# A hybrid recurrence and attention trunk on one core: the products of x1 with the compression, query and gate weights, as seven 2x2 block products in place of eight

## The chip, the cores and the metric

One core of a Trainium2 chip runs the whole program. The metric is the device time of one launch in microseconds (us), the median of the runs shown. Engines go by the profile's names: PE (TensorE) multiplies, DVE (VectorE) and ACT (ScalarE) do the elementwise work, POOL (GpSimd) and SP issue transfers (DMAs). Each engine takes its instructions in the program's order and waits on semaphores that others raise.

## The reference, cut to what matters

```python
x1 = x + rglru_layer(x, ...)                 # ends in y @ w_out_a
h  = rms_norm(x1, norm_kv)
ckr = h @ w_dkv                              # 256 columns for k and v, 64 for the rotated keys
c_kv = rms_norm(ckr[..., :256], kv_norm)
k_rope = apply_rope(ckr[..., 256:], cos, sin)
h  = rms_norm(x1, norm_b)
u  = h @ w_in_b                              # 384 query columns, 8 x 128 gate columns
c_q = rms_norm(u[..., :384], q_norm)
gate = u[..., 384:]
q  = c_q @ w_uq                              # 128 plain and 64 rotated columns for each of 8 heads
o  = causal attention over k = c_kv @ w_uk with k_rope, v = c_kv @ w_uv
out = rms_norm(x1 + (o * silu(gate)) @ w_out_b, final_norm)
```

Sequence 1024, model width 1024, recurrence width 1280, all in float32.

## The kernel before, in words

**Layout.** A tile holds 128 channels by the sequence, which is worked in two halves of 512 columns (`hs(h)`). To multiply float32 values, every operand is split in two parts by `hl` (lines 79 to 81): ACT copies it rounded (`hi`, line 80), DVE takes the difference (`lo`, line 81). A product of a 128x128 weight block with 128x512 data is then three matmuls (`mm3`, lines 111 to 114: hi*hi, hi*lo, lo*hi); `mmt` strings them over the 128-channel blocks k into one PSUM tile. Weights come through `wload` (line 83): a load by SP (line 89), a gain by DVE where one is wanted (line 93), then the split. Their raw tiles have 2 buffers, the parts 4. Large tiles are pages, 36 of 128x1024 in one pool.

**Phase A** is the recurrence; its ten results `ys` stand as 20 pages. The change leaves it alone.

**Phase B** (lines 457 to 491) makes x1 = x + y @ w_out_a, eight tiles of 128 channels by ten k-blocks. `out_a` (line 460) loads a piece of x (`xr`, 2 buffers), adds it to the PSUM tile (line 464), splits x1 into the pages `xs1` (line 465), stores x1 (line 466, POOL's queue) and adds its squares to `acc1`.

**Phase C** (lines 493 to 631) multiplies x1 by 14 weight tiles of 128 columns: 2 for k and v, 1 for the rotated keys, 3 query tiles, 8 gates. Each takes 2 halves x 8 k-blocks x 3 matmuls of 128x512. The row norm of x1 is a factor for each column, so it is applied behind the product (`byr`, line 160; `rstd`, line 137, makes the root). Between the products stand: the rotation of the keys (lines 556 to 575), the norms and splits of c_kv and c_q (`normed`, line 520), and the query rotation of two groups of four heads (lines 606 to 623), whose parts go to DRAM (`qsd`) to be read back for each head. Six gates follow the query rotation. A gate is sigmoid on ACT (line 597), times itself on DVE (line 598), stored to `gd`. The first weights of phase C are loaded and split while phase B still multiplies (`wq_`, `wnext`), and the first product takes 7 of its 8 k-blocks before the last tile of x1 is wanted.

**Attention** (line 633 on) goes head by head. Its PSUM pool `pss` is opened when phase C's pool `psp` closes, in the same banks. First come head 0's plain queries and keys (tiles `pm`, line 112 to 114 by `kq`), then the scores `s`, whose rotated part reads `qs`, loaded from `qsd`.

**What sets the order.** A scheduler orders each engine's instructions by their dependences and priorities when the program is built; `wload` raises the priority of weights by 100. A pool's memory that is given on (`pa.close()`, `pc.close()`) makes the next user wait for the last readers of what lay there.

## Time and profile before

| | us |
|---|---|
| median of 3 runs | 900.16 (900.0 to 900.78) |
| span of the profiled execution, first to last instruction | 896.9 |
| matmuls in the profile, PE busy | 4410, 874.6 |
| DVE busy, ACT busy | 645.0, 447.6 |

The profiled execution's own time is not given beside its span; the median lies 3.3 us above the span, and that difference is taken as what lies around it. Rows of groups read: line, engine, operation, written tile <- read tiles, shape and count, then busy us, mean ns of one, and the idle time before them with what ended it. Rows of stretches give for each engine the busy us and the instruction count, then the clock granted to PE. Timeline rows give the start, the length, and the instruction. A mean length is from start to end of one instruction; engines overlap the end of one with the start of the next, so the step from start to start is shorter.

### The profile page before, as it was taken

The page shows a single profiled execution, that of the slowest core. Times are in us where ns is not written, and L with a number is a line of the kernel's source. Part 1 is how long each engine was busy: PE and PEld are TensorE (multiplying, and loading weights), DVE is VectorE, ACT ScalarE, POOL GpSimd, SP SyncE. Part 2 cuts the span into 40 slices and gives each one's busy share as a digit, 9 for nine tenths or more (in the row PEclk, how much of TensorE's full clock was granted, in tenths as well). Part 3 has the DMA queues.
Part 4 walks back from the last instruction along what each step waited for, and adds up shares of the span by engine and source line. Part 5 has one row for each costly group of instructions (what it writes and reads, how often), then busy time and mean ns, then how long its engine had stood idle before and what let it go on. Part 6 is the DMA issues. An engine that isn't in the chain of part 4 may idle for free.

```text
span 896.9 us, 12070 instructions
## 1 busy us (share of the span) xinstructions
PE 874.6 (98%) x4410; PEld 743.4 (83%) x4410; DVE 645.0 (72%) x1192; ACT 447.6 (50%) x765; POOL 67.9 (8%) x125
## 2 busy tenths in 40 slices
PE   7999999999999999999999999999999999999993
PEld 5788888888887888888888888989998998888993
DVE  7988787777777545559599636978887887774552
ACT  6457777777787323233343225645565554331221
POOL 3001110011000100001003000000000000010000
PEclk9999999999999999999999999999999999999997
DMA  7333333333221644412125324223231317565131
GB/s 266 101 105 94 98 91 103 97 106 101 75 58 53 196 119 135 142 38 74 51 97 211 141 86 132 77 74 106 75 109 66 115 60 280 189 228 171 64 103 48
DMA packets 49612, 101.66 MB, mean 113 GB/s; under 512 B 6160, under 2 KB 16272, under 8 KB 49552
## 3 DMA queue, kind: packets, MB, share of 16 engines
q1 hardware_dynamic: 35952, 66.40, 23.3%
q0 software_dynamic: 13328, 34.22, 11.4%
q8 instruction: 35, 0.57, 0.3%
q10 hardware_dynamic: 272, 0.26, 0.1%
q14 instruction: 25, 0.20, 0.1%
HBM read 77.26 MB, written 23.07 MB: 112 GB/s over the span
## 4 chain that ended last, share of the span: by engine, by line
PE 70%; DVE 11%; issue 9%; ACT 6%; DMA 2%; POOL 1%; SPq 0%; DVEq 0%; POOLq 0%; ACTq 0%
PE ps L113 11%; PE ps L114 11%; PE ps L112 10%; PE pm L114 5%; PE pm L113 5%; PE pm L112 5%; PE pm L710 3%; DVE t L356 2%; PE pm L727 2%; PE pm L726 2%; PE s L691 2%; PE s L693 2%; PE s L694 2%; PE s L692 2%; PE pm L725 2%
## 5 line engine op out<-in xcount | busy, mean ns | idle before, releaser
L113 PE MATMUL ps<-pg,wh 128*128 128x512 f32 x728 | 284.2, 390 | 3.2 <-DVE pg L260 2.9
L112 PE MATMUL ps<-pg,wh 128*128 128x512 f32 x728 | 283.4, 390 | 2.0 <-ACT wh L80 1.3
L114 PE MATMUL ps<-pg,wl 128*128 128x512 f32 x728 | 283.7, 390 | 0.3 <-DVE wl L81 0.3
L113 PEld LDWEIGHTS ps<-pg,wh 128*128 128x128 f32 x728 | 136.7, 188 | 34.4 <-DVE pg L260 5.7
L112 PEld LDWEIGHTS ps<-pg,wh 128*128 128x128 f32 x728 | 136.6, 188 | 31.2 <-ACT wh L80 1.4
L114 PEld LDWEIGHTS ps<-pg,wl 128*128 128x128 f32 x728 | 136.7, 188 | 29.2 <-DVE wl L81 1.2
L80 ACT ACTIVATE wh<-wr 128x512 fp32r<-128x512 f32 (+2 forms) x85 | 48.3, 571 | 64.8 <-PE ps L113 48.4
L80 ACT ACTIVATE pt<-pm 128x512 fp32r<-128x512 f32 (+2 forms) x96 | 44.4, 490 | 59.4 <-PE pm L710 57.4
L81 DVE TENSOR_TENSOR wl<-wr,wh 128x512 fp32r<-128x512 f32 (+2 forms) x85 | 52.1, 615 | 27.4 <-ACT wh L80 27.0
L700 ACT ACTIVATE pg<-s,m 128x128 f32<-128x128 f32 (+3 forms) x64 | 47.5, 743 | 46.0 <-DVE m L697 41.2
L112 PE MATMUL pm<-pg,pg 128*128 128x256 f32 (+1 forms) x192 | 61.9, 323 | 0.0
L113 PE MATMUL pm<-pg,pg 128*128 128x256 f32 (+1 forms) x192 | 61.6, 321 | 0.0
L114 PE MATMUL pm<-pg,pg 128*128 128x256 f32 (+1 forms) x192 | 61.4, 320 | 0.0
L81 DVE TENSOR_TENSOR pt<-pm,pt 128x512 fp32r<-128x512 f32 (+2 forms) x96 | 50.6, 548 | 1.9 <-ACT pt L80 1.8
L697 DVE TENSOR_REDUCE m<-s 128x1 f32<-128x128 f32 (+3 forms) x64 | 48.1, 754 | 1.0
L80 ACT ACTIVATE pg<-pg 128x512 fp32r<-128x512 f32 x46 | 29.0, 632 | 39.3 <-DVE pg L410 17.8
L356 DVE SCALAR_TENSOR_TENSOR t<-xb,vec,t 128x512 f32<-128x512 f32 x60 | 44.7, 746 | 0.4
L710 PE MATMUL pm<-ident,pg 128*128 128x128 f32 x288 | 42.4, 274 | 0.3 <-DVE pg L702 0.3
L112 PEld LDWEIGHTS pm<-pg,pg 128*128 128x128 f32 x192 | 36.6, 191 | 2.6 <-issue 0.2
L113 PEld LDWEIGHTS pm<-pg,pg 128*128 128x128 f32 x192 | 36.6, 191 | 2.6 <-issue 0.2
L114 PEld LDWEIGHTS pm<-pg,pg 128*128 128x128 f32 x192 | 36.6, 191 | 2.5 <-DVE pg L756 0.3
L690 PE MATMUL s<-pg,pg 128*128 128x512 f32 (+2 forms) x96 | 37.1, 387 | 0.9 <-ACT pg L700 0.9
(188 smaller groups left out, 1611.9 us busy)
## 6 DMA issues: line engine op xcount, KB each, us to landing
wr<-wina SPq DMA_DIRECT2D x40, 256.0 KB, 2.8
wh<-wina POOLq DMA_DIRECT2D x36, 256.0 KB, 3.0
wr<-winc SPq DMA_DIRECT2D x28, 256.0 KB, 2.6
ysd<-pg POOLq DMA_DIRECT2D x12, 512.0 KB, 3.2
pg<-ysd SPq DMA_DIRECT2D x12, 512.0 KB, 8.2
wr<-wouta SPq DMA_DIRECT2D x16, 256.0 KB, 2.7
xr<-xT SPq DMA_DIRECT2D x16, 256.0 KB, 3.0
x1d<-t POOLq DMA_DIRECT2D x16, 256.0 KB, 3.4
```

The source lines that it names most:

```text
L80: A.activation(out=hi, in_=src, func=AF.Copy)
L81: V.tensor_tensor(out=lo, in0=src, in1=f(hi), op=ALU.subtract)
L112: T.matmul(out=ps, lhsT=w[0], rhs=r[0], start=first, stop=False)
L113: T.matmul(out=ps, lhsT=w[0], rhs=r[1], start=False, stop=False)
L114: T.matmul(out=ps, lhsT=w[1], rhs=r[0], start=False, stop=last)
L356: V.scalar_tensor_tensor(out=xc, in0=xb[:, j:j + HW], scalar=cwv[j], in1=xc, op0=ALU.mult, op1=ALU.add)
L690: T.matmul(out=sc[:, c], lhsT=q[0][:, ql], rhs=k[0][:, c], start=True, stop=False)
L691: T.matmul(out=sc[:, c], lhsT=q[0][:, ql], rhs=k[1][:, c], start=False, stop=False)
L692: T.matmul(out=sc[:, c], lhsT=q[1][:, ql], rhs=k[0][:, c], start=False, stop=False)
L697: V.tensor_reduce(out=m, in_=sc, axis=AX.X, op=ALU.max, negate=True)
L700: A.activation(out=p_[:, 0:nk], in_=sc, func=AF.Exp, bias=m, accum_out=l)
L710: T.transpose(out=ps[:, (b - b0) * P:(b - b0 + 1) * P], in_=p_[:, b * P:(b + 1) * P], identity=ident)
```

## The change

**Factors in place of x1's parts.** Phase B works the tiles of x1 in pairs (j, j+4). Of each pair and its two halves, four pieces b11, b12, b21, b22 of 128x512, `factors` makes seven operands (three of them differences, one a further sum, on DVE) and splits each into its `fx` pages, 28 pages in place of 16. The last pair (3, 7) is multiplied together, k-block by k-block in four PSUM tiles, so that the pages of `ys` come free one after the other.

**Weights in place.** `wpair` loads four 128x512 pieces of two weight tiles, puts the gain on with ACT (four instructions for each piece), makes the four combinations with DVE and splits seven operands. The tiles `wa` lie in a pool that opens when phase B's pool `ta` closes.

**Seven products in place of eight.** `pair` multiplies seven operands by seven, four k-blocks each, in four PSUM tiles, three of which take a second product on top of what they hold. DVE combines the results (`v2`, `u3` and lines 603 to 612) and applies the row norm. The first pair takes three of its four k-blocks first.

**Moved behind the gates:** the splits of c_q and c_kv (`parts`), the rotation of the keys with the loads of its tables, and the query rotation of the first four heads. The second group of the query rotation moves into the attention, in head 1. Gates use ACT's Silu in place.

```diff
-    xs1 = [(page(), page()) for _ in range(NKT)]
+    fx = [[None, None] for _ in range(7)]
...
+    def factors(j, b11, b12, b21, b22):
+        fput(0, j, b11)
+        t1 = diff(b11, b12, ALU.subtract)
+        fput(1, j, t1)
+        t2 = diff(b22, t1, ALU.add)
+        fput(2, j, t2)
+        fput(3, j, diff(b12, b22, ALU.subtract))
+        fput(4, j, b21)
+        fput(5, j, diff(b21, t2, ALU.subtract))
+        fput(6, j, b22)
...
+    def wblock(m, h):
+        t = tcp.tile([P, HW], F32, tag="wa", bufs=NWA, name=nm("wa"))
+        nc.sync.dma_start(out=t, in_=winc[m, :, hs(h)])
+        for k in range(4):
+            c = slice(k * P, (k + 1) * P)
+            A.activation(out=t[:, c], in_=t[:, c], func=AF.Copy, scale=g[:, 4 * h + k:4 * h + k + 1])
+        return t
...
+    def wpair(m):
+        with tc.high_priority(offset=WPC):
+            a11, a21, a22 = wblock(m, 0), wblock(m + 1, 0), wblock(m + 1, 1)
+            split(a11)
+            s = wp.tile([P, HW], F32, tag="wr", bufs=2, name=nm("ws"))
+            add(s, a21, a22)
+            split(s)
+            add(s, s, a11)
+            split(s)
+            add(a11, a11, a21)
+            split(a11)
+            a12 = wblock(m, 1)
+            split(a12)
+            split(a22)
+            add(a12, a12, s)
+            split(a12)
...
+    def pair(m, dst, early=None, after=None):
+        w = wpair(m)
+        a, c, b, d = (pst() for _ in range(4))
...
+            if i == 0:
+                A.activation(out=q1, in_=a, func=AF.Copy)
+            elif i == 2:
+                V.tensor_tensor(out=v2, in0=b, in1=q1, op=ALU.subtract)
+            elif i == 3:
+                V.tensor_tensor(out=u3, in0=d, in1=v2, op=ALU.add)
+        V.tensor_tensor(out=dst[1][1], in0=u3, in1=c, op=ALU.subtract)
+        byr(dst[1][1], dst[1][1], r1[:, hs(1)])
+        fmul(a, w[4], 4, range(4), False)
+        byr(dst[0][0], a, r1[:, hs(0)])
+        fmul(d, w[5], 5, range(4), False)
+        V.tensor_tensor(out=dst[1][0], in0=d, in1=v2, op=ALU.add)
+        byr(dst[1][0], dst[1][0], r1[:, hs(0)])
+        fmul(c, w[6], 6, range(4), False)
+        V.tensor_tensor(out=dst[0][1], in0=c, in1=v2, op=ALU.subtract)
+        byr(dst[0][1], dst[0][1], r1[:, hs(1)])
...
+    for j in range(0, NH, 2):
+        gts = [page(F32) for _ in range(2)]
+        pair(6 + j, [halves(g) for g in gts])
...
+        if j == 0:
+            normed(qt, qacc, QN, SCALE)
...
+    cq = parts(qt)
+    ckv = parts(kvt)
...
+    nc.sync.dma_start(out=cs, in_=rope[0])
+    nc.sync.dma_start(out=sn, in_=rope[1])
+    for j in range(4):
+        i = j ^ 1
+        DQ.dma_start(out=krs[32 * j:32 * j + 32, :], in_=krt[32 * i:32 * i + 32, :])
...
+    for h in range(2):
+        qrope(0, h, pst)
     pc.close()
...
+    rwork = [lambda h=h: qrope(1, h, pm) for h in range(2)]
...
+        for wl, n in ((rwork, int(hd == 1 and qb in (2, 5))), ...
```

**Between phase B and phase C, ACT.** `wh` are a weight's rounded parts, `wr` its raw tile, `t` pieces of x1, `acc` the sum of squares. Before, ACT's rows at the end of phase B are:

```order
L80 ACTIVATE wh_3089<-wr_3088 128x512
L80 ACTIVATE wh_3198<-wr_3197 128x512
L80 ACTIVATE wh_3205<-wr_3204 128x512
L80 ACTIVATE pg_2432<-t_3169 128x512
L471 ACTIVATE t_3174<-t_3169 128x512
L80 ACTIVATE th_3324<-acc_2434 128x512
```

Now, with `wa` the weight pieces of the first pair (line 545 the gains, lines 82 and 475 the splits and squares):

```order
L475 ACTIVATE t_3206<-t_3203 128x512
L82 ACTIVATE pg_3013<-t_3203 128x512
L82 ACTIVATE pg_2987<-t_3211 128x512
L82 ACTIVATE pg_2993<-t_3215 128x512
L82 ACTIVATE pg_2999<-t_3219 128x512
L82 ACTIVATE pg_3009<-t_3225 128x512
L82 ACTIVATE th_3357<-acc_2418 128x512
L545 ACTIVATE wa_3239<-wa_3239,vec 128x128 x4
L545 ACTIVATE wa_3245<-wa_3245,vec 128x128 x4
L545 ACTIVATE wa_3251<-wa_3251,vec 128x128 x4
L82 ACTIVATE wh_3257<-wa_3239 128x512
```

The splits of the first weights of phase C stood ahead of the last piece of x1; the first one now stands behind all the factors of the last pair and behind twelve gain instructions. The load of wa_3239 waits in the program for the difference t_3225, the last of the factors, because its tile lies where `ta` had its own.

**From phase C into the attention, PE.** Before, the last product of the last gate is followed by head 0's queries:

```order
L112 MATMUL ps_4505<-pg_2432,wh_4409 128x512
L113 MATMUL ps_4505<-pg_2433,wh_4409 128x512
L114 MATMUL ps_4505<-pg_2432,wl_4410 128x512
L112 MATMUL pm_4566<-pg_3494,wh_4552 128x512 [waits DVE_49,Activation_49]
L113 MATMUL pm_4566<-pg_3495,wh_4552 128x512
```

Now, with `pg_4498` to `pg_4511` the parts of c_q and ps_4606 the last tile of the query rotation:

```order
L114 MATMUL ps_4606<-pg_4510,wh_4562 128x512
L115 MATMUL ps_4606<-pg_4511,wh_4562 128x512
L116 MATMUL ps_4606<-pg_4510,wl_4563 128x512
L114 MATMUL pm_4674<-pg_4498,wh_4660 128x512 [waits DVE_49,Activation_49]
L115 MATMUL pm_4674<-pg_4499,wh_4660 128x512
```

The DVE instruction waited for was a `byr` two products back (line 160, of ps_4416); it is now line 711, the last reading of ps_4606. **DVE at the same place.** Before, around the last gate's scalings:

```order
L160 SCALAR_TENSOR_TENSOR pg_4475<-ps_4505,acc_2434 128x512
L81 TENSOR_TENSOR wl_4618<-wr_4616,wh_4617 128x512
L598 TENSOR_TENSOR pg_4475<-pg_4475,tg_4531 128x512
L81 TENSOR_TENSOR pg_4560<-pm_4566,pg_4559 128x512
L81 TENSOR_TENSOR wl_4656<-wr_4654,wh_4655 128x256
```

Now the same engine has the keys' rotation (lines 692 to 694) and the query rotation (lines 710 to 712) there; the last twelve rows up to the one PE waits for are:

```order
L712 TENSOR_TENSOR pg_4587<-pg_4587 128x512
L710 TENSOR_TENSOR pg_4596<-ps_4567,pg_4534 128x512
L83 TENSOR_TENSOR pg_4588<-pg_4587,pg_4588 128x512
L711 TENSOR_TENSOR pg_4596<-ps_4568,pg_4533 128x512
L712 TENSOR_TENSOR pg_4596<-pg_4596 128x512
L710 TENSOR_TENSOR pg_4625<-ps_4605,pg_4533 128x512
L83 TENSOR_TENSOR pg_4597<-pg_4596,pg_4597 128x512
L711 TENSOR_TENSOR pg_4625<-ps_4606,pg_4534 128x512
L712 TENSOR_TENSOR pg_4625<-pg_4625 128x512
L710 TENSOR_TENSOR pg_4634<-ps_4605,pg_4534 128x512
L83 TENSOR_TENSOR pg_4626<-pg_4625,pg_4626 128x512
L711 TENSOR_TENSOR pg_4634<-ps_4606,pg_4533 128x512
```

Between line 611, which reads phase C's last product, and this last row stand 34 DVE instructions, both included. In SP's order the two table loads (lines 684 and 685) stand behind four weight loads of the attention, two of them for `wuv`.

More of the change, by code (lines that the diff above doesn't have):

```diff
@@ L490, in trunk @@
+    x1s = [out_a(3 + 4 * i, h, po[i][h]) for i in range(2) for h in range(2)]
+    factors(3, *x1s)
     pa.close()
     pc = ExitStack()
[L494 to L501 removed]
@@ new lines, in wpair, with split, add @@
+    def wpair(m):
+        def split(t):
+            hi = wp.tile([P, HW], F32R, tag="wh", bufs=4, name=nm("wh"))
+            lo = wp.tile([P, HW], F32R, tag="wl", bufs=4, name=nm("wl"))
+            hl(t, hi, lo)
+            out.append((hi, lo))
+        def add(o, x, y):
+            V.tensor_tensor(out=o, in0=x, in1=y, op=ALU.add)
+        out = []
+        with tc.high_priority(offset=WPC):
[13 more added lines that the diff above has]
+            split(a12)
+        return out
@@ L626, in trunk @@
+    qrw = {}
+    for h in range(2):
+        qrope(0, h, pst)
     pc.close()
```

257 lines of the change are left out of this document (129 added, 128 removed).

## Prediction

> **What bounds the kernel now.** I read the page's first part, then the stretches, then PE's waits, then its timeline. The first part shows PE as the bound; the commonest group of matmuls lasts 390 ns each:
>
> ```profile
> PE 874.6 (98%) x4410; PEld 743.4 (83%) x4410; DVE 645.0 (72%) x1192; ACT 447.6 (50%) x765; POOL 67.9 (8%) x125
> L114 PE MATMUL ps<-pg,wl 128*128 128x512 f32 x728 | 283.7, 390 | 0.3 <-DVE wl L81 0.3
> ```
>
> The stretches tell which engine would be next (columns: stretch, length, busy us and count of PE, PEld, DVE, ACT, POOL, then the granted clock):
>
> ```profile
> 292.00:376.00 84.00, 84.00 (x373) 69.57 (x371) 42.07 (x70) 27.06 (x48) 7.56 (x14) 1.00 0.49 150
> 386.00:440.00 54.00, 54.00 (x240) 44.62 (x239) 43.00 (x69) 21.63 (x35) 3.93 (x8) 1.00 0.19 59
> 500.00:545.00 45.00, 45.00 (x200) 37.27 (x199) 19.27 (x31) 10.99 (x19) 2.66 (x5) 1.00 0.29 99
> 600.00:700.00 100.00, 100.00 (x606) 89.75 (x605) 83.08 (x183) 56.44 (x128) 3.19 (x6) 1.00 0.26 86
> ```
>
> In phase B (292 to 376), the early part of phase C (386 to 440), the late gates (500 to 545) and the attention (600 to 700) PE never rests. DVE is half busy in phase B, four fifths busy early in phase C, 43% in the late gates, and 83% in the attention. Here are all the waits of PE on other engines from 270 to 570, so through both changes of stage that the diff touches:
>
> ```profile
> PE ps L112 <- ACT pg L80: 0.8, 1, 0.8
> PE ps L114 <- DVE wl L81: 0.3, 1, 0.3
> ```
>
> So both changes of stage are covered today: fewer matmuls pay in full, and anything that uncovers a change of stage costs in full. What a matmul is worth is not its length, since one starts before the last has ended. Between these two rows of PE's timeline lie 117 steps:
>
> ```profile
> 290.09 0.39 PE L112 MATMUL ps<-pg,wh 128*128 128x512 f32 x1
> 316.61 0.39 PE L112 MATMUL ps<-pg,wh 128*128 128x512 f32 x1
> ```
>
> (316.61 - 290.09) / 117 = 0.2267 us is the price of one.
>
> **Part 1, fewer products.** 14 weight tiles at 2 x 8 x 3 = 48 products are 672; seven pairs at 7 x 4 x 3 = 84 are 588. That removes 84: 84 x 0.2267 = **-19.0 us**, all on the path. The eight rotated-query products are moved, not saved.
>
> **Part 2, the stop between phases B and C.** Rows for the DVE, ACT and DMA steps:
>
> ```profile
> L464 DVE TENSOR_TENSOR t<-ps,xr 128x512 f32<-128x512 f32 x16 | 11.0, 689 | 19.7 <-PE ps L114 16.7 <-DMA xr<-xT 2.9
> 485.15 0.69 DVE L618 TENSOR_TENSOR t<-t,t 128x512 f32<-128x512 f32 x1
> 485.75 0.69 DVE L617 TENSOR_TENSOR t<-ps,sn 128x512 f32<-128x512 f32 x1
> 486.35 0.68 DVE L617 TENSOR_TENSOR t<-ps,cs 128x512 f32<-128x512 f32 x1
> L80 ACT ACTIVATE wh<-wr 128x512 fp32r<-128x512 f32 x43 | 26.9, 629 | 47.8 <-PE ps L113 36.2 <-DMA wr<-wouta 4.9 <-ACT t L471 3.3
> L259 ACT ACTIVATE pg<-pg,vec 128x1024 fp32r<-128x1024 f32 x7 | 8.0, 1136 | 0.7 <-DMA pg<-xT 0.7
> L259 ACT ACTIVATE pg<-pg,vec 128x512 fp32r<-128x512 f32 x2 | 1.4, 722 | 2.2 <-DMA pg<-xT 2.2
> L80 ACT ACTIVATE pt<-pm 128x128 fp32r<-128x128 f32 x16 | 4.4, 274 | 22.4 <-PE pm L710 20.4 <-PE pm L727 2.0
> wr<-winc SPq DMA_DIRECT2D x28, 256.0 KB, 2.6
> xr<-xT SPq DMA_DIRECT2D x16, 256.0 KB, 3.0
> ```
>
> DVE takes 0.69 for a 128x512 row and starts the next after 0.60. ACT takes 0.63 for a split. Count from T0, when the last product of phase B can be read. Its four PSUM tiles end 3 products apart, so the first add (line 469) starts 9 x 0.2267 = 2.0 before T0 and ends at -1.3. There are two `xr` buffers, so the third piece of x is loaded only then, lands 3.0 later, and the third add starts at about +1.8. From it to the difference t_3225 stand 12 DVE rows: 11 x 0.60 + 0.69 = 7.3, and 0.2 for ACT's splits between: +9.3. SP's load of wa_3239 waits for that row: +2.6 makes 11.9. Then ACT's 12 gains of 128x128. No row shows one; two others bound it: the plain copy at 274 ns, and the scaled form, which goes from 722 ns at 512 columns to 1136 at 1024, so 0.81 ns a column: 722 - 384 x 0.81 = 412 at 128. Rows overlap by about 0.1 on DVE; I take 0.30 (0.17 to 0.41), nearest to the copy, which has the shape: 3.6, to 15.5. The split's rounded part 0.63 and its difference 0.69 follow: 16.8. PE's third product needs the last; it would have started 0.45 - 0.16 = 0.3 after T0. PE loses **+16.5** (15 with the short gain, 21 with the long one and with a 5.9 landing, the slow row of part 4).
>
> Before, the splits of these weights stood ahead of x1's last tile, so nothing of this chain showed. What could hide it now is other PE work: there is none, since the first product of the pair needs this weight.
>
> **Part 3, inside the pairs.** A pair is 84 products, 19.0 us. DVE owes it 7 splits, 4 combinations and 9 rows for results: 20 x 0.60 = 12.0. The late gates are covered, with 7 us to spare. The first pairs also carry the squares and norms: from the first pair's first split to the q norm's last row stand 135 DVE rows, 81 us, beside 412 products, 93.4 us. That is 87%, about what 386 to 440 shows now (43.0 of 54.0) without a wait. But the work is bunched. In the first pair two weight splits stand ahead of `u3` on DVE and wait for buffers that the fourth product holds; by the steps above `u3` ends some 4.4 after it, and PE has 14 products, 3.2, until it writes on the tile that `u3` reads: 1.2, and 0.3 for the first differences. The two ones-products of a norm stand in PE's order ahead of blocks, with their parts one and two rows late on DVE: 0.7 and 0.4, again for the q norm. Together 3.7; rows that read the row before take 0.69 instead of 0.60, so I take **+5** (0 to 12; the upper end is a norm's DVE rows, 10 x 0.60, uncovered twice). On ACT a gate's Silu has a table load beside it, 1.3 each:
>
> ```profile
> L146 ACT ACT_TABLE_LOAD x2 | 2.6, 1283 | 0.0
> ```
>
> ACT was 22 us busy in the 54 from 386, so it is costed at nothing, and at 1.3 if it stood uncovered. The factors in phase B are nothing as well, but for the last pair: 28 splits and 16 differences for 16 splits, so 28 more DVE rows, 16.8 us, where DVE had 42 of 84 idle; uncovered they would be in part 2 already.
>
> **Part 4, the stop before the attention.** Two transfers matter that were long done before:
>
> ```profile
> cs<-rope SPq DMA_DIRECT2D x1, 512.0 KB, 5.9
> sn<-rope SPq DMA_DIRECT2D x1, 512.0 KB, 6.4
> qsd<-tl POOLq DMA_DIRECT2D x8, 256.0 KB, 2.4
> qs<-qsd SPq DMA_DIRECT2D x32, 128.0 KB, 2.8
> kb<-ka POOLq DMA_DIRECT2D x8, 64.0 KB, 3.3
> ```
>
> Count from T1, the last product of the last pair. PE still has the 36 rotated-query products: 36 x 0.2267 = 8.2. Its next, head 0's first `pm` product, waits for line 711's last reading of ps_4606, the 34th DVE row from T1. The first 12 are this pair's last result, splits of c_q and c_kv and four weight splits. The two `wuv` splits there wait for a buffer that the rotated-query weights hold until 8.2; ACT's rounding and DVE's difference put their end at 9.6. SP issues the two tables behind the `wuv` loads, at about 3.8 and 4.1, so they land at 9.7 and 10.5. The swapped keys go through POOL behind the last gate's store, five issues and 3.3 of landing, about the same time. Then 22 rows are left, the second of which needs `sn`: 10.5 + 20 x 0.60 + 0.69 = 23.2, and some 0.9 for rows that need the row just before them: 24.1. PE, free at 8.0, loses 16.1. The stores of the last parts and head 0's load of them, 2.4 + 2.8 behind that, run beside the 30 products of head 0's queries and keys, 6.8 us, and cost 0.3. Sum **+16.4** (12.5 if no row waits for anything: 33 x 0.60 + 0.69 - 8.0; 20.5 with the last 22 at 0.69 and the landings 2 later).
>
> **Part 5, head 1.** The other four heads' rotation brings 16 DVE rows, 9.6 us, into the attention of head 1, some 40 us, where DVE is 83% busy, 33 of 40: 2.8 too much if none could be done late. Most can, since these heads come later: **+1** (0 to 5, twice the 2.8 less what runs on).
>
> **Part 6, the clock.** What a stop does to the granted clock (third number from the right; DVE's, ACT's and POOL's busy times stand left of it):
>
> ```profile
> 18.71 0.50 PE L113 MATMUL ps<-pg,wh 128*128 128x512 f32 x1 [2.95 <-DVE pg L260]
> 16.00:17.00 1.00, 0.00 (x0) 0.00 (x0) 1.00 (x1) 0.11 (x1) 1.00 (x1) 1.00 0.53 192
> 883.00:883.50 0.50, 0.05 (x1) 0.00 (x0) 0.00 (x0) 0.38 (x1) 0.00 (x0) 1.00 0.00 0
> 884.50:885.00 0.50, 0.00 (x0) 0.00 (x0) 0.47 (x2) 0.00 (x0) 0.00 (x0) 0.64 0.00 0
> 885.00:886.00 1.00, 0.00 (x0) 0.00 (x0) 1.00 (x2) 0.00 (x0) 0.93 (x2) 0.50 0.00 0
> ```
>
> An idle time of 2.95 left the clock at 1.00; after the last big products, at 883.05, it fell to 0.50 within 1.7. Both stops are longer, so PE starts again at half clock. No row shows how soon full clock returns. At half clock a time t of work loses t / 2; I take 1.6 us of it: 0.8 a stop, **+1.6** (0 to 6). The Trainium skill, "TensorE: Matmul & The Clock Gate", Part 1: The HAM clock gate (the "warmup" mystery), says that an idle window of about 3.4 us halves the clock and about 3.4 us of sustained work restores it, and so speaks against a change that opens stops. By it each stop would lose 1.7, an estimate, and the sum be 1.8 higher; its idle window fits the 2.95 that cost nothing, its return no row here shows.
>
> **Sum.** 896.9 - 19.0 + 16.5 + 5.0 + 16.4 + 1.0 + 1.6 = 918.4 for the span. The median of the runs lies 3.3 above the span of before: 921.7, so **922**.
>
> **The rivals.** A, the other side: the hand-over of memory costs little at both places. For it: today pools change hands at both, and PE waited 0.8 and 0.3. Against: today nothing that PE needs next stands behind the hand-over. Without both stops and their clock, 900.2 - 19.0 + 6.0 = 887, and 881 with the pairs covered too. It decides if both stops and the clock together cost under 11 us where I count 34.5.
>
> B, a product is worth its 390 ns: 84 x 0.39 = 32.8 saved, 13.8 more than I took, 908. The 117 steps speak against it; PE's uncounted starts at stage changes are too few to make it.
>
> C, the second stop alone is covered, because the scalings and rotations run ahead of PE: 922 - 16.4 - 0.8 = 904.8. For it: the late gates leave DVE 7 us in a pair. Against: the tables are asked for after T1, and line 692 waits for them.
>
> D, DVE bounds the pairs: if each of the 135 rows takes its whole 0.69, as rows that read the row before do, they make 93.2 us beside 93.4 of products, and the bunches (ends of part 3, 4 and 5) come out in full: 7 + 4 + 4 more, 937; half of that 930.
>
> That the change doesn't do what it says is excluded: PE's order has 84 rows fewer.
>
> **How the numbers follow.** My forecast 0.70, A 0.05, B 0.05, C 0.06, D 0.14. The low ends of the terms give 909 together, all high ends 946; 908 to 938 leaves out A, C and the upper end of D and of the forecast, under 0.2. The measurement can tell 0.2%, 1.8 us: faster is A, 0.05; same 0.02, a middle of A and C; slower 0.93.
>
> **What would show it.** Two PE waits of 15 to 21 and 12 to 20 us where the first has DVE's `wl` of the first pair and the load `wa<-winc` behind t_3225 as its chain, and the second ends on line 711; the granted clock 0.50 behind each; matmuls 84 fewer with the same step; DVE above 85% between. Wrong would be a stop under 8 us, a chain that ends on other work, or PE in the pairs idle for more than 12 us.

## The result, and the profile after

The changed kernel takes 928.59 us, the median of 4 runs (927.28 to 929.32). The kernel before took 900.32 beside it (900.0 to 900.78, 4 runs). The ratio is 1.031, with a 95% interval of 1.0295 to 1.0324: slower by 3.1%. The forecast was 922, with a range of 908 to 938. The profiled execution spans 925.5 where the one before spanned 896.9, so there are 28.6 us to place.

The first part of the profile after, and the group of matmuls that answers to the one shown in the prediction:

```profile
PE 865.2 (93%) x4326; PEld 732.0 (79%) x4326; DVE 687.9 (74%) x1260; ACT 505.6 (55%) x919; POOL 66.0 (7%) x121
L116 PE MATMUL ps<-pg,wl 128*128 128x512 f32 x688 | 269.5, 392 | 0.1
```

84 matmuls are gone (4410 to 4326), and yet PE's share falls from 98% to 93%. PE waits now. All its waits on other engines from 270 to 600:

```profile
PE pm L114 <- DVE pg L711: 19.3, 1, 19.3
PE ps L114 <- ACT wh L82: 18.1, 1, 18.1
PE ps L143 <- ACT th L82: 1.4, 3, 0.7
PE ps L114 <- ACT pg L82: 0.8, 1, 0.8
```

The first two are the stops that the prediction named. The stretches (columns as in the prediction) show that between and behind them PE rests little. 400 to 500 lies in the pairs, 620 to 640 in the attention:

```profile
400.00:500.00 100.00, 98.59 (x432) 80.28 (x431) 90.32 (x143) 72.51 (x158) 2.14 (x4) 1.00 0.23 76
620.00:640.00 20.00, 18.18 (x111) 15.60 (x110) 18.88 (x37) 11.54 (x25) 2.90 (x6) 1.00 0.44 141
```

DVE is busy 90 of 100 in the pairs, and PE waits 1.4 there. So the pairs go at PE's pace with little to spare.

**The first stop, step by step.** These are rows of the timeline of all engines after, in order of time; the first is the last product of phase B:

```profile
370.10 0.39 PE L116 MATMUL ps<-pg,wl 128*128 128x512 f32 x1
372.19 0.69 DVE L469 TENSOR_TENSOR t<-ps,xr 128x512 f32<-128x512 f32 x1 [0.42 <-DMA x1d<-t]
374.25 0.69 DVE L469 TENSOR_TENSOR t<-ps,xr 128x512 f32<-128x512 f32 x1 [1.37 <-DMA xr<-xT]
380.28 0.68 DVE L483 TENSOR_TENSOR t<-t,t 128x512 f32<-128x512 f32 x1
383.70 2.64 ACT L545 ACTIVATE wa<-wa,vec 128x128 f32<-128x128 f32 x8 [0.69 <-DMA wa<-winc]
386.75 1.28 ACT L545 ACTIVATE wa<-wa,vec 128x128 f32<-128x128 f32 x4 [0.41 <-DMA wa<-winc]
387.93 0.61 ACT L82 ACTIVATE wh<-wa 128x512 fp32r<-128x512 f32 x1
388.60 0.79 PE L114 MATMUL ps<-pg,wh 128*128 128x512 f32 x1 [18.11 <-ACT wh L82]
```

Read it as the chain in which each row sets the next free. The third and fourth pieces of x1 are added, the differences follow, the last of them (380.28) ends at 380.96, the load that waits for its memory has landed by 383.70, twelve gains follow, then the split, then PE. From 370.10 to 388.60, less one step of 0.227, PE loses 18.3.

**The second stop.** Rows of DVE's, POOL's and PE's timelines after. 529.38 is the last pair's last result, so about T1 of the prediction, 537.19 the last rotated-query product:

```profile
529.38 0.68 DVE L611 TENSOR_TENSOR pg<-ps,v 128x512 f32<-128x512 f32 x1
532.79 1.95 POOL L688 DMA_DIRECT2D pg<-pg  x4
536.28 0.69 DVE L83 TENSOR_TENSOR wl<-wr,wh 128x512 fp32r<-128x512 f32 x1 [1.21 <-ACT wh L82]
537.19 0.39 PE L116 MATMUL ps<-pg,wl 128*128 128x512 f32 x1
538.41 0.69 DVE L83 TENSOR_TENSOR wl<-wr,wh 128x512 fp32r<-128x512 f32 x1 [1.43 <-ACT wh L82]
542.03 0.69 DVE L692 TENSOR_TENSOR pg<-pg,pg 128x512 f32<-128x512 f32 x1 [2.93 <-DMA pg<-pg]
556.09 0.68 DVE L711 TENSOR_TENSOR pg<-ps,pg 128x512 f32<-128x512 f32 x1
556.92 0.77 PE L114 MATMUL pm<-pg,wh 128*128 128x512 f32 x1 [19.34 <-DVE pg L711]
```

DVE stands idle for 1.2 and 1.4 ahead of the splits of the two value weights (536.28 and 538.41), which come before the rotation in its order. It reaches the first rotation row 12.6 after 529.38, because the swapped keys landed only then, and ends line 711 at 556.77, 27.4 after it. PE loses 556.92 - 537.19 - 0.23 = 19.5. The landings are longer than the rows of before, by the profile's list of DMA issues after:

```profile
pg<-rope SPq DMA_DIRECT2D x2, 512.0 KB, 8.8
pg<-pg POOLq DMA_DIRECT2D x4, 128.0 KB, 7.0
```

**The clock.** Stretches behind the two stops (the granted clock is third from the right):

```profile
388.00:390.00 2.00, 1.40 (x3) 1.05 (x4) 1.79 (x3) 1.99 (x7) 0.00 (x0) 0.50 0.01 3
392.00:394.00 2.00, 2.00 (x9) 1.59 (x9) 1.09 (x2) 1.83 (x6) 0.00 (x0) 0.88 0.42 131
556.00:558.00 2.00, 1.08 (x3) 0.92 (x4) 1.46 (x3) 0.47 (x1) 0.82 (x2) 0.50 0.52 193
560.00:562.00 2.00, 2.00 (x10) 1.60 (x9) 0.69 (x1) 0.60 (x1) 0.00 (x0) 1.00 0.78 270
```

After the first stop nine products take from 388.60 to 392.56, 3.96 where full clock needs 9 x 0.227 = 2.04: 1.9 lost. After the second, six products from 556.92 to 559.62 lose 1.3.

The whole difference of the two profiled executions, in us, counted along PE's order (the same product, before and after):

| part | predicted | measured |
|---|---|---|
| 84 products fewer | -19.0 | -19.0 |
| stop 1 | +16.5 | +18.3 |
| inside the pairs | +5 | +2.6 |
| stop 2 | +16.4 | +19.5 |
| half clock behind both | +1.6 | +3.2 |
| the other heads' rotation | +1 | +2.9 |
| ahead of phase B's end, and the rest | 0 | +1.1 |
| sum | +21.5 | +28.6 |

The first row is 84 steps of 0.2267, a price that a run below checks. The 2.9 is the attention, from head 0's first product to the last norm's first, less the 36 moved products and the half clock: 353.23 - 340.85 - 8.16 - 1.34. The 1.1 is 1.5 that has gathered in the first 37 us, ahead of anything that the change touches, less 0.4 of small differences behind it.

### The profile page after: what moved, and what is told of

It is laid out like the page before. It is cut to its first block, busy times and chain, and to the rows that moved or that the text cites. A ratio compares the mean times of both kernels' runs of the same rounds, so it can differ in the third digit from the quotient of the medians.

```text
span 925.5 us, 12118 instructions
## 1 busy us (share of the span) xinstructions
PE 865.2 (93%) x4326; PEld 732.0 (79%) x4326; DVE 687.9 (74%) x1260; ACT 505.6 (55%) x919; POOL 66.0 (7%) x121
## 4 chain that ended last, share of the span: by engine, by line
PE 59%; DVE 15%; issue 12%; ACT 7%; DMA 4%; POOL 1%; SPq 0%; POOLq 0%; DVEq 0%; ACTq 0%
PE ps L115 7%; PE ps L114 7%; PE ps L116 7%; PE pm L114 6%; PE pm L115 5%; PE pm L116 5%; PE pm L804 3%; PE pm L821 2%; PE pm L820 2%; PE s L785 2%; PE pm L819 2%; PE s L788 2%; PE s L786 2%; PE s L787 2%; PE s L784 2%
## 5 line engine op out<-in xcount | busy, mean ns | idle before, releaser
L114 PE MATMUL ps<-pg,wh 128*128 128x512 f32 x688 | 270.1, 394 | 19.7 <-ACT wh L82 18.7
L115 PE MATMUL ps<-pg,wh 128*128 128x512 f32 x688 | 270.4, 393 | 1.5 <-DVE pg L262 1.4
L116 PE MATMUL ps<-pg,wl 128*128 128x512 f32 x688 | 269.5, 392 | 0.1
L114 PEld LDWEIGHTS ps<-pg,wh 128*128 128x128 f32 x688 | 130.4, 190 | 49.0 <-ACT wh L82 19.4
L115 PEld LDWEIGHTS ps<-pg,wh 128*128 128x128 f32 x688 | 130.2, 189 | 31.3 <-DVE pg L262 3.4
L116 PEld LDWEIGHTS ps<-pg,wl 128*128 128x128 f32 x688 | 130.2, 189 | 28.0 <-DVE wl L83 1.2
L82 ACT ACTIVATE pg<-pg 128x512 fp32r<-128x512 f32 x56 | 34.7, 629 | 50.1 <-DVE pg L412 18.1
L114 PE MATMUL pm<-pg,wh 128*128 128x512 f32 x92 | 36.6, 398 | 19.3 <-DVE pg L711 19.3
L82 ACT ACTIVATE wh<-wr 128x512 fp32r<-128x512 f32 (+2 forms) x57 | 30.7, 542 | 27.9 <-PE ps L115 14.4
L83 DVE TENSOR_TENSOR wl<-wr,wh 128x512 fp32r<-128x512 f32 (+2 forms) x57 | 32.7, 577 | 13.8 <-ACT wh L82 13.7
L545 ACT ACTIVATE wa<-wa,vec 128x128 f32<-128x128 f32 x112 | 36.1, 390 | 9.5 <-DMA wa<-winc 9.2
L83 DVE TENSOR_TENSOR pg<-pg,pg 128x512 fp32r<-128x512 f32 x56 | 38.0, 683 | 2.1 <-ACT pg L82 1.5
L114 PEld LDWEIGHTS pm<-pg,pg 128*128 128x128 f32 x192 | 36.6, 191 | 2.6 <-issue 0.2
```

What stands on the lines that cost most here:

```text
L82: A.activation(out=hi, in_=src, func=AF.Copy)
L83: V.tensor_tensor(out=lo, in0=src, in1=f(hi), op=ALU.subtract)
L114: T.matmul(out=ps, lhsT=w[0], rhs=r[0], start=first, stop=False, skip_group_check=more)
L115: T.matmul(out=ps, lhsT=w[0], rhs=r[1], start=False, stop=False, skip_group_check=more)
L116: T.matmul(out=ps, lhsT=w[1], rhs=r[0], start=False, stop=last, skip_group_check=more)
L545: A.activation(out=t[:, c], in_=t[:, c], func=AF.Copy, scale=g[:, 4 * h + k:4 * h + k + 1])
```

## The experiments

My theory is the prediction's: a product is worth 0.227 on the path; each stop is a chain of hand-overs of memory and of DVE rows that PE has nothing to cover; and each stop halves the clock. The rivals are that DVE's sum of rows bounds the pairs or the stops whatever their order, and that products cost another price. Times are medians with their ratio to the kernel before, run on the same chip (899.64, 899.92, 900.31 and 899.89 in the four groups of runs, 900.32 beside the changed kernel). So a difference of two medians from different groups is uncertain by up to 0.7 for that alone.

### The price of a product

The first block product of six pairs is made twice; the second overwrites the first. 6 x 12 = 72 products more:

```diff
                 fmul(ps, w[i], i, range(4), True)
+                if i == 0:
+                    fmul(ps, w[i], i, range(4), True)
```

> The changed kernel, with the first block product of six pairs (all but the first) made twice, 72 matmuls more, the result unchanged. Theory (PE bounds the pairs and a matmul costs its step of 0.2267 us): 72 x 0.2267 = 16.3 more, less at most the 2.4 us that PE waits in these pairs: 942.5 to 945. Rival (DVE bounds the pairs, so that products are free in part): at most 5 more, under 934.

943.47 (942.99 to 944.18), ratio 1.0491 (1.0473 to 1.0508). That is 14.9 above the changed kernel, 0.207 a product, where 0.227 was the step. The traces say where the rest is: from the first pair's first product to the first rotated-query product the profiled execution takes 157.4 where the changed kernel's takes 140.5. Of these 16.9, 0.8 is a longer half clock behind the first stop, and 16.1 for 72 products is 0.224 each; the first stop ahead of them happened to be 1.4 shorter (16.7 for 18.1). PE bounds the pairs: were DVE the bound, the 16 us would have vanished beside it. The saving of 84 products is real, 17 to 19 us.

### The first stop, memory

The first pair's four weight pieces go into two pages instead of tiles in the memory that the last factors free:

```diff
-            a11, a21, a22 = wblock(m, 0), wblock(m + 1, 0), wblock(m + 1, 1)
+            if m == 0:
+                a11, a21, a22, a12 = wblock(m, 0, 0), wblock(m + 1, 0, 1), wblock(m + 1, 1, 2), wblock(m, 1, 3)
...
+    fw = [page(F32) for _ in range(2)]
```

> The changed kernel, but the four weight pieces of the first pair lie in two pages of phase B instead of the memory that ta gives on, so they are loaded, scaled and split while phase B multiplies. Theory (the stop of 18.1 us between phases B and C is one chain: last factor, memory given on, load, twelve gains, split): the stop goes, with its 1.9 of half clock; what is left is the last factors' own splits, which PE wants from 8.2 us after phase B and which end some 3.5 to 4 later than that: 928.6 - 18.3 - 1.9 + 4 = about 912. Rival (DVE is the bound there: the 14 rows of factors and the 12 of the first weights take the same time wherever they stand): only landing and gains go, 6 to 8 us, about 921.

916.43 (914.09 to 917.05), ratio 1.0183 (1.0167 to 1.0198): 12.2 less than the changed kernel. The wait of 18.1 is gone; the longest piece left of it, and the DVE row at which this kernel's timeline shows why:

```profile
PE ps L114 <- ACT pg L82: 2.7, 2, 1.9
```

```profile
368.78 0.69 DVE L560 TENSOR_TENSOR ws<-pg,pg 128x512 f32<-128x512 f32 x1 [7.65 <-ACT pg L548]
```

DVE sits idle for 7.65 ahead of that row, for gains on pieces that SP could load only from 362.5 on, when their pages came free, and from 368.8 to 389 it then works almost without a gap. So memory was the cause of the stop, and the pages that I chose were still handed over late. The time lies midway between the theory's 912 and the rival's 921: what is left here is DVE's queue. The next kernel takes two pages that are free long before, and loads and scales the pieces ahead of x1's middle tiles:

```diff
+    def early_blocks():
...
+            nc.sync.dma_start(out=t, in_=winc[m, :, hs(h)])
...
+    fb = early_blocks()
     for j in range(1, 3):
```

> The changed kernel, with the first pair's weight pieces in the two pages that are free before the second pair of x1's tiles, so that landing, gains and sums stand ahead of the last products of phase B, in DVE's idle time, and not among the last factors. Theory (what was left of the first stop with the pieces in late pages, 5.6 us and its clock, is DVE's queue after phase B's last product: 33 rows there without a gap, 11 of them the first weights'): with seven of these rows gone the factors' splits end before PE asks for them, at 8 to 10 us after phase B, and the stop is 0 to 1: about 909. Rival (the third and fourth piece of x, loaded only when their buffers are free, set the end of the factors): the same as with late pages, 916.

911.21 (909.93 to 913.32), ratio 1.0127 (1.0113 to 1.0141): 17.4 less than the changed kernel. What is left at this place:

```profile
PE ps L114 <- ACT q L614: 2.9, 1, 2.9
```

That is ACT's copy of the first product. Its target `q1` lies in the same handed-over memory, so it waits for the last factor's reading (a run below moves it, and this wait goes). Half clock follows it (0.50 at 385 to 387).

### The second stop, transfers and order

The tables and the swapped keys are asked for ahead of everything else at this place, the swap through SP:

```diff
+    cs, sn, krs = page(F32), page(F32), page(F32)
+    with tc.high_priority(offset=400):
+        nc.sync.dma_start(out=cs, in_=rope[0])
...
+            nc.sync.dma_start(out=krs[32 * j:32 * j + 32, :], in_=krt[32 * i:32 * i + 32, :])
     cq = parts(qt)
```

> The changed kernel, but the two rotation tables and the swapped keys are asked for ahead of the attention's weights (priority), the swap on SP's queue. Theory (of the 19.3 us stop before the attention, DVE's idle time until the tables and swap have landed, 12.6 us after the last gate's last product, is one part, and DVE's rows are the rest): DVE runs on without a gap, 35 rows of 0.65 from the last product, stop about 15, time about 924. Rival (the landing is covered: the rotation waits for the wuv weights' buffers and the products anyhow): no change, 928 to 929.

922.19 (921.47 to 922.79), ratio 1.0251 (1.0236 to 1.0266): 6.4 less than the changed kernel. The wait, 19.3 before the edit, is now

```profile
PE pm L114 <- DVE pg L712: 14.0, 1, 14.0
```

From the last pair's last result to line 712's last row DVE now has no gap, so the 14 that are left are DVE rows. The 5.3 were its idle time: 2.9 and 0.3 for the landings, and 1.2 and 1.4 for the splits of the value weights, which now stand behind the keys' rotation. So the landings themselves were about 3 of it, and the order the rest. Next, with the tables first as here (now through POOL), the parts of c_q and the query rotation go ahead of the last pair's end, the keys' rotation and c_kv's parts behind them, the first value weights lose their priority, and the rotation's weights get memory of their own two pairs earlier (with 5 `wa` tiles instead of 6 to make room):

```diff
+        if j == 4:
+            rotw()
...
+    with tc.high_priority(offset=400):
+        cq = parts(qt)
...
+    with tc.high_priority(offset=400):
+        for h in range(2):
+            qrope(0, h, pst)
+    R1, R2 = page(), page()
```

> The changed kernel, with the stop before the attention taken apart: tables on POOL's queue and swap on SP's ahead of the attention's weights, the first rotation's weights in memory of their own and loaded before the last two pairs, c_q's parts and the query rotation with priority over the last pair's last products, the keys' rotation and c_kv's parts behind the query rotation. Theory (the stop is the queue of DVE rows that stand behind the last product): only about five rows stand between the last product and the row that PE waits for, stop 3 to 6, its clock loss of 1.3 gone: 928.6 - 19.5 - 1.3 + 5 = about 913. Rival (DVE is the bound: the same rows take the same time, and PE waits for them at another place, in the last pairs or at the first scores): 922 or more.

927.30 (923.86 to 929.05), ratio 1.0303 (1.028 to 1.0327). A miss, and an instructive one:

```profile
PE ps L143 <- ACT th L82: 6.5, 2, 6.0
PE pm L114 <- DVE pg L719: 6.0, 1, 6.0
PE s L800 <- ACT pg L810: 2.8, 1, 2.8
```

The stop did fall, from 19.3 to 6.0. A new one stands in its place at the norm of c_q: ACT's order has changed, so that the split the norm needs stands behind a root, two table loads, a Silu and four gains. Two things of this edit could have changed it, the room taken from the weights and the rotation's weights loaded two pairs early; no run separates them, but with both taken back (next section) this wait is gone. The clock is at 0.50 behind each of the three waits (476 to 480, 550 to 554, 564 to 568). The prediction had costed ACT's table loads at nothing because ACT was idle enough on average; by its order in this kernel it wasn't.

### Both stops mended

The early pieces and the early rotation together, with all 6 `wa` tiles, `v2` in one buffer, and the rotation's weights loaded ahead of the last pair:

```diff
-        q1, v2, u3 = tmp("q1"), tcp.tile([P, HW], F32, tag="v2", bufs=2, ...), tmp("u3")
+        q1, v2, u3 = tmp("q1"), tcp.tile([P, HW], F32, tag="v2", bufs=1, ...), tmp("u3")
...
+        if j == 6:
+            rotw()
```

> The changed kernel with both stops mended: the first pair's weights in the two free pages; c_q's parts, the tables (POOL's queue), the swapped keys (SP's) and the query rotation with priority over the last pair's last products, the rotation's weights in memory of their own, loaded ahead of the last pair with the six weight buffers kept, so that the q norm's rows keep their place on ACT; the keys' rotation and c_kv's parts behind the query rotation. Theory (the two stops are all that lies between the saved products and a gain): first stop 0 to 1, second 3.7, then some 3.5 at the first keys' products, whose parts stand 20 DVE rows behind the last pair, and 1 of clock: 928.6 - 19.7 - 20.8 + 8.2 = about 896, under the kernel before by 3 to 4. Rival (DVE's rows have to be done somewhere, and ACT's order puts them in PE's way elsewhere, as the 6 us at the q norm did): 905 or more.

903.86 (902.86 to 904.56), ratio 1.0041 (1.0027 to 1.0054). 24.7 of the 28.3 are back, so the two stops are the cause of the loss. But the forecast of 896 is missed. PE's longest waits are these:

```profile
PE pm L114 <- DVE pg L737: 4.8, 1, 4.8
PE ps L114 <- ACT q L614: 2.9, 1, 2.9
PE s L818 <- ACT pg L828: 2.8, 1, 2.8
```

They are 10.5 together where the forecast had 7 to 8. As much was missed by the clock, which had been put at 1 in all: behind the first stop eight steps take 3.5 (385.07 to 388.57) where full clock needs 1.8, and behind the second eleven take 4.7 (527.34 to 532.08) where it needs 2.5.

### What is left

Four more edits went at these three. In the first, `q1` of the first pair goes to a buffer of the weights, the score tiles take the PSUM banks of the rotation in place of the projections' tiles, the last pair's Silus run on whole pages, and head 0's weights lose their priority:

```diff
+        q1, v2, u3 = wp.tile([P, HW], F32, tag="wr", bufs=2, ...) if early else tmp("q1"), ...
...
+    pss.tile([P, S], F32, tag="s", name=nm("s"))
```

> The kernel with both stops mended (903.86) still waited 2.9 for ACT's copy of the first product (its target lies in memory that the last factor frees) and 4.8 for the last rotated row, each with some 1.6 to 2 of half clock behind. Here the copy goes to a page-free buffer of the weights, the score tiles take the PSUM banks of the rotation in place of the projections' tiles, and the last pair's Silus run on whole pages. If PE was held by these two hand-overs: 4.5 less for the first, 899.4, and up to 2 less for the second, so 897.5 to 899.5. The rival: DVE's rows bound both places (weights of the last pieces, parts of c_kv), the waits only change their names, and the time stays at 902 or more.

903.97 (902.9 to 905.41), ratio 1.0041 (1.0028 to 1.0053). The rival was right: the waits change their names. The copy's wait is gone, but at the second stop PE now starts on head 0's queries and stops at its keys:

```profile
PE pm L114 <- ACT pg L82: 3.7, 1, 3.7
PE s L820 <- ACT pg L830: 3.0, 1, 3.0
```

The second edit takes this kernel and puts c_kv's parts ahead of the keys' rotation (one line moved up; head 0's weights have their priority again).

> As the run before it, but the parts of c_kv stand ahead of the keys' rotation on ACT and DVE. If the keys' products of head 0 wait for c_kv's parts, which come 6 DVE rows (3.6 us) earlier: 1 to 3 less than the run before it. The rival: the scores need the keys' rotation just behind, DVE's sum of rows is the same, and the time is within 0.5 of the run before it.

902.41 (901.32 to 903.95, 11 runs), ratio 1.0025 (1.0016 to 1.0034): 1.6 less, inside the theory's 1 to 3. The ratios' intervals overlap, so the trace is the better witness: the wait for c_kv's parts fell from 3.7 to 1.2, and the next one in PE's order is for the keys' product parts:

```profile
PE s L821 <- DVE pg L83: 2.2, 1, 2.2
```

DVE worked from 517.7 to 537.4 without a gap in this run. So here it is DVE's sum of rows that bounds. The third edit takes two rows out of that stretch: the splits of the value weights come behind the keys' rotation, and the last Silus and the stores move with them. It was put on record together with the fourth, which its expectation calls the run before it:

```diff
+    for i in range(2):
+        A.activation(out=gts[i], in_=gts[i], func=AF.Silu, bias=zb, scale=1.0)
...
-        uh, ul = wload(wuv[pair], 512, pri=pair > 0)
+            raw, u2 = wp.tile([P, 512], F32, tag="wr", bufs=2, name=nm("wr")), page()
...
+            hl(raw, uh, ul)
```

> As the run before it, but without the rows on POOL and ACT's copies: only the splits of value weights, the last Silus and the stores are moved. By the bound on DVE's rows 2 x 0.60 come out: 1.2 less than 902.41, so 901.2, and 0.8 above the run before it. The rival: these splits were no part of the chain, and the time stays at 902.4.

901.04 (900.36 to 904.59, 12 runs), ratio 1.0018 (1.001 to 1.0027): 1.4 less by the medians, where two rows are 1.2. But the kernel before is 0.4 faster beside this run too, and the intervals of the two ratios overlap, so the price of these rows is not shown. It is the best of these versions, and 0.2% slower than the kernel before. The fourth edit adds to it that two results of the last pair and their scalings leave DVE for ACT and POOL:

```diff
+        if last:
+            A.activation(out=dst[1][0], in_=d, func=AF.Copy)
+            G.tensor_tensor(out=dst[1][0], in0=dst[1][0], in1=v2, op=ALU.add)
```

> From the kernel with c_kv's parts first (902.41): two result rows of the last pair and their two scalings leave DVE (ACT copies the PSUM tile, POOL adds and multiplies), the two splits of value weights come behind the keys' rotation, the last Silus too, and the rotated queries' stores go through SP. If DVE's rows bound the hand-over: 4 rows and two splits, 6 x 0.60 = 3.6, come out of the stretch ahead of the first scores, of which ACT's copy, that waits for a product ahead of a rotation's split in its queue, gives some 1.5 back: 2 less, 900.4, level with the kernel before. The rival: the order on ACT holds DVE as long as DVE's own order did, and the time is 902 or more.

905.29 (904.14 to 907.79), ratio 1.0063 (1.0051 to 1.0076): 4.3 more than without it. The rival's number holds. In the trace PE waits 3.5 for the rotation's last row where it waits 1.4 without the edit. The rival's reason is not what makes the difference: DVE did wait 1.6 for a split on ACT, but at that place it waits 1.8 for a product without the edit. What else the trace shows no theory had. DVE's timeline of this kernel, while POOL works and after, and POOL's:

```profile
518.18 1.36 DVE L83 TENSOR_TENSOR pg<-pg,pg 128x512 fp32r<-128x512 f32 x1 [1.63 <-ACT pg L82]
519.47 0.68 DVE L747 TENSOR_TENSOR pg<-ps,pg 128x512 f32<-128x512 f32 x1
520.07 1.18 DVE L760 TENSOR_TENSOR pg<-pg,pg 128x512 f32<-128x512 f32 x1
521.17 1.76 DVE L748 TENSOR_TENSOR pg<-pg 128x512 f32<-128x512 f32 x1
522.85 1.75 DVE L761 SCALAR_TENSOR_TENSOR pg<-pg,sgn,pg 128x512 f32<-128x512 f32 x1
526.92 0.68 DVE L748 TENSOR_TENSOR pg<-pg 128x512 f32<-128x512 f32 x1
```

```profile
517.71 1.28 POOL L630 TENSOR_TENSOR pg<-pg,v 128x512 f32<-128x512 f32 x1 [18.44 <-ACT pg L629]
519.08 1.62 POOL L162 TENSOR_TENSOR pg<-pg,acc 128x512 f32<-128x512 f32 x1
520.66 1.73 POOL L637 TENSOR_TENSOR pg<-pg,v 128x512 f32<-128x512 f32 x1
522.46 1.59 POOL L162 TENSOR_TENSOR pg<-pg,acc 128x512 f32<-128x512 f32 x1
```

The same row of line 748 lasts 1.76 beside POOL's rows and 0.68 when they are over; the row that reads PSUM (line 747) keeps its 0.68. The four long rows lost 1.36 + 1.18 + 1.76 + 1.75 - 4 x 0.68 = 3.3, more than the four rows that had been taken from DVE would have lasted (2.4). How the 4.3 divides is not shown: the execution profiled without the edit was that kernel's slowest (904.59), the one with it the fastest of its five (904.14), and in these two PE is level again 20 us behind the wait. The Trainium skill, "SBUF — State Buffer", SBUF: two separate sides, says that the two engines share a pair of SBUF ports as an exclusive lock, which a DVE operation with two SBUF inputs takes against a POOL operation that reads SBUF; the trace agrees, 1.76 against 0.68.

### The clock by itself

66 dummy products fill the first stop of the changed kernel; they are written into the first pair's first PSUM tile and overwritten there:

```diff
+            for n in range(66):
+                T.matmul(out=a, lhsT=fx[0][0][0][:, 0:P], rhs=fx[0][0][0][:, hs(0)], start=n == 0, stop=n == 65)
```

> The changed kernel, with 66 products more between phase B and the first pair, of a factor with itself into the PSUM tile that the first real product overwrites; 66 x 0.2267 = 15.0 us of the 18.1 us in which PE waits anyway. Theory (PE restarts at half clock because it was idle): the 1.9 us of half clock behind the first stop go, 926 to 927, and the granted clock stays 1.00 there. Rival (the slow start belongs to the waited-for operands or to the length of the stop, not to idleness): no change, 928.6.

926.36 (924.39 to 928.56), ratio 1.0294 (1.0279 to 1.0309). Inconclusive: PE still waited 2.3 behind the dummies, and in the profiled execution, the slowest of the four at 928.56, the clock fell in spite of 15 us of work just ahead:

```profile
388.00:390.00 2.00, 1.38 (x3) 1.04 (x4) 1.77 (x3) 2.00 (x7) 0.00 (x0) 0.64 0.05 17
390.00:392.00 2.00, 2.00 (x6) 1.55 (x5) 1.80 (x4) 2.00 (x7) 0.00 (x0) 0.51 0.00 0
```

With 75 dummies instead:

> The changed kernel with 75 dummy products in the first stop (17.0 us of its 18.3), which are written into the first pair's first PSUM tile and overwritten there; nothing else changes. PE then idles about 0.3 ahead of the first real product, where it idled 2.3 with 66 of them. If the halved clock comes from the idle time just ahead: granted clock 1.00 behind the stop and 1.9 less than the changed kernel, 926.7. The rival, that the clock falls for another reason (the change of work at the hand-over): 0.5 to 0.65 again in 388 to 392, and 928.6.

926.42 (925.15 to 927.43), ratio 1.0286 (1.0272 to 1.03): 2.2 less than the changed kernel. The wait is 0.9, and in the profiled execution the clock stays up:

```profile
388.00:390.00 2.00, 1.70 (x6) 1.12 (x7) 1.81 (x4) 2.00 (x7) 0.00 (x0) 1.00 0.01 2
```

So it is the idle time that halves the clock, and not the change of work; at the first stop that is worth about 2 us, as forecast. The other three runs with 66 dummies took 924.4 to 926.5; a wait of 2.3 that goes either way would fit that, but they left no trace. The last section comes back to it.

## Why the prediction came out as it did

The direction, and the mechanism, were right: 928.6 lies inside the range, both stops stand where they were put, behind line 82 with the load of `wa` as its chain and behind line 711, and mending both brings back 24.7 to 27.5 of the 28.3. By the prediction's own steps:

**Part 1, the products.** -19.0 holds. 72 added products cost 14.9, 0.207 each, so rival B with its 0.39 a product is out.

**Part 2, stop 1.** 18.3 against 16.5, in the bounds of 15 to 21. The chain was right link by link: the third add at +1.8 of T0 came at +1.7, the first load's landing of 2.6 fits the row that waits for it, and the gain, of which no row was at hand, takes 2.64 / 8 = 0.33 in the string of eight and 0.30 in one of sixteen (4.80, the run with late pages), where I took 0.30. Two links were left out. The fourth piece of x waits for its buffer as the third does, and landed 1.4 late (the 1.37 on the second L469 row); the third weight piece landed 0.4 late. I had counted rows behind the third add as if nothing but DVE set their pace.

**Part 3, the pairs.** +2.6 against +5, in its bounds. The waits at the norms (L143, 1.4 together) are the part that showed; the wait at `u3`, the largest single piece, never came. DVE was 90% busy from 400 to 500, above the 85% that I gave as a sign, and still PE bounded, as the added products showed.

**Part 4, stop 2.** 19.5 against 16.4. The count of 22 rows in the rotation was right, and they took 14.7 where I had about 14.2. What failed is the landing: I took 3.3 for the swapped keys and about 6 for the tables from transfers of before that had fewer others beside them, and the keys' copies were half as large there (64 KB for 128). Here they run together with the last gates' stores and the weights of head 0, and took 7.0 and 8.8. Size alone is not it: in the run with the rotation first the same copies took 2.7 through SP, and with the tables first 6.9 through SP. That makes the first rotation row start at 12.6 and not at 10. With the tables asked for first DVE did not wait for them at all, so the step was not only late but avoidable.

**Part 5, the other heads' rotation.** +2.9 against +1, inside 0 to 5. The price falls where DVE has the second half of these rows (lines 710 to 712, from 630.7 to 636.7): PE's 1.8 of idle time is at 634.7 and 639.8, as head 2's first scores begin, a little later than I put it.

**Part 6, the clock.** 3.2 against 1.6. The step "0.8 a stop" was mis-sized: no row showed the return, and I took it short. It was 1.9 and 1.3 in the changed kernel. The estimate of 1.7 a stop that the prediction worked out from the Trainium skill ("TensorE: Matmul & The Clock Gate", Part 1: The HAM clock gate) comes to 3.4, and the trace agrees with it better than with mine.

So the miss is a sum of terms mostly of one sign: the two stops 4.9, the clock 1.6, the attention 1.9, and 1.1 outside the change, less 2.4 in the pairs. That the pairs' surplus hid so much of the rest is luck. These 7.1 of the span are 6.6 in the times, since the median lies 3.1 above this span and 3.3 above that of before, and 921.7 was rounded up. The 3.3 is not what lies around the span, as I took it: each run of the changed kernel takes 1.8 more than its own span, and the other 1.5 is that the profiled execution of before was faster than the median. The profiled one of the changed kernel is its fastest too, so the two nearly cancel. Of the rivals, A (cheap hand-overs) and C (the second stop covered) are out by the two waits. D, DVE as the bound of the pairs, predicted a time of 930 to 937 that is near; but its mechanism is out, by the added products. DVE's sum of rows does bound at one place that D did not name: the hand-over into the attention, once the waits for memory and landings are gone and DVE has no gap there.

One thing stays open: whether seven products can be made to pay here. With both stops mended as far as these edits went, 901.0 to 902.4 still holds waits of 1 to 2 us at the second hand-over, and it is not shown that they can all be covered. A plain compression with Strassen products in the gates alone was not tried.

## What to carry to other kernels

A rewrite that saves work on the bounding engine also moves the points at which memory changes hands; before counting the saving, list for each such point the first instruction behind it, what frees its operands, and the chain of loads, gains and splits that then stands bare. Where the saving is 19 us and a chain is 18, everything hangs on whether buffers can be had one stage earlier. And take a transfer's landing from one of the same size, in a stretch in which as much is under way as there will be: rows of a quieter stretch gave 6 for 8.8.

## What the runs showed of the hardware

**A wait of the same length halves the clock or doesn't.** At one place near the start, which is the same in all these kernels, PE waits some 2.3 to 2.9 us. Two of the kernels above, the early rotation and the first pair's pieces in late pages, by PE's timeline and the stretch behind it:

```profile
19.19 0.50 PE L115 MATMUL ps<-pg,wh 128*128 128x512 f32 x1 [2.25 <-DVE pg L262]
```

```profile
21.00:22.00 1.00, 1.00 (x4) 0.71 (x4) 1.00 (x1) 0.26 (x1) 0.44 (x1) 0.50 0.78 264
```

```profile
20.19 0.50 PE L115 MATMUL ps<-pg,wh 128*128 128x512 f32 x1 [2.40 <-DVE pg L262]
```

```profile
21.00:22.00 1.00, 1.00 (x6) 0.83 (x5) 0.96 (x5) 1.00 (x2) 0.29 (x1) 1.00 0.00 0
```

2.25 halved it, 2.40 didn't, and the 2.95 of the kernel before didn't either. In the 14 profiled executions of this document the clock fell to 0.50 behind this wait in 11, with waits from 2.25 to 2.95, and stayed in 3 (1.17, 2.40, 2.95). So for an idle time of 2 to 3 us the length does not decide. The Trainium skill, "TensorE: Matmul & The Clock Gate", Part 1: The HAM clock gate (the "warmup" mystery), says that the window runs free and isn't started by the kernel, so that it would matter when the wait falls; that fits, but no run here tests it. That it takes an idle window of about 3.4 us does not fit the 2.25.

**POOL and DVE slow each other** when both read SBUF: DVE's 0.68 became up to 1.76. POOL's rows took 1.59 to 1.73 there, and 1.28 where DVE was idle for the first 0.5 of it.

**The gain of 128x128 on ACT** takes 0.30 to 0.33 a step (4.80 for sixteen, 2.64 for eight), inside the bounds of 0.17 to 0.41 that a plain copy and longer gains had set.
